# A decoder layer step: [high | low] operand for the sample tile, layer norm straight into the feed-forward accumulator, cache copy in pieces

## The chip, the core and the metric

One core of one Trainium2 chip. The time is that of one execution of the whole program on the device, in microseconds (us); a kernel's figure is the median of several runs. The engines are called as the profile calls them: PE (TensorE), PEld (its weight loads), DVE (VectorE), ACT (ScalarE), POOL (GpSimd) and SP (SyncE, which issues the DMA transfers here).

## What is computed

One inference step of a decoder trunk of one layer, for a prompt of 1024 tokens and a sample group of 8 requests with 8 new tokens each, which share the weights. All of it is float32. Cut to what matters here:

```python
x = layer_norm(x, ln_emb_g, ln_emb_b)
a_b, a_c, a_h, g_q, ..., n_kv, n_win, n_gate = split_in(x @ w_in)
...
win_all = concatenate([win_buf, win_new]); win_state = win_all[:, t:]
mix = concatenate([y_a, y_b, y_c]) @ w_out
x = layer_norm(ALPHA * x + mix, ln1_g, ln1_b)
gate, val = split(x @ w_up, 2)
gate, ffn_new = causal_dwconv(gate, ffn_buf, ffn_conv_w)
x = layer_norm(ALPHA * x + (silu(gate) * val) @ w_down, ln2_g, ln2_b)
```

The model width is 1024, the feed-forward width 2816. `win_state` of the sample group is an output of 8 x 512 rows; 504 rows of each request are a plain copy of the cache (4.03 MB in all), 8 are new.

## The kernel before

The 1088 tokens are nine tiles: tiles 0 to 7 of 128 prompt tokens and **tile 8 of the 64 sample tokens** (`rows_of`). Products are made float32-exact by splitting both operands into a high and a low part: `mm3` (L196 to L202) issues three matmuls for each 128 of the contraction, high x high (L200), low x high (L201) and high x low (L202), all into one PSUM tile. The token tile is the stationary operand in four projections, and there tile 8 has 64 stationary columns:

- `rows` in phase_a (L303 to L322), `pn`: 800 columns of w_in in natural layout, two halves of 400 columns, 8 steps of the contraction each. Its weights come in eight raw pieces (`nraw`, L288), cast to `nh` on ACT (L296) and split to `nl` on DVE or POOL (L297). `transpose_split` (L164 to L173) makes the transposed high and low operands of a token tile.
- `phase_part` (`pwq`): the first 4 of 8 contraction steps of w_out, two halves of 512 columns, run as filler within the attention part; its result goes to x_d.
- `phase_out` (`pwo`, L1607 to L1650): the other 4 steps, then the first layer norm by sums (`layer_norm_sums`, tag "1"; L143 on DVE, L144 on ACT, L145 on POOL). The result `xo` is stored to ax_d in DRAM (L1640) and transposed for the next part (`finish`, tpx).
- `down` in phase_ffn (`pd`, L1730 to L1755): w_down, two halves of 512 columns.

The feed-forward part first loads the accumulator `acc` from ax_d, a load per tile (L1668), and behind the last of these it issues the copy of the window cache to its output, one transfer of 4.03 MB from DRAM to DRAM (L1679 to L1681). It then goes over 22 blocks of 128 feed-forward channels. `up_block` makes the gate (`pug`) and value (`puv`) products in chunks of 384, 384 and 320 tokens with the weights stationary, copies the gate out of PSUM (`fg`, L1709, ACT), convolves it on DVE, and splits the product into `hh` (ACT) and `hl` (POOL, L1721). Weights come as raw tiles `wrf` (L182; cast `whf` on ACT L191, split `wlf` on POOL L192) and `wdr` (L1723; `dh`, `dl`), which share two raw buffers. After every two blocks, `down` adds both blocks' product to `acc` for tiles 0 to 8 in order: ten such groups and a last one, in which the second layer norm follows: by sums for tiles 0 to 6, and by `layer_norm_end` with a store for each half for the last two (`ENDS = 2`), tiles 7 and 8.

The order of the instructions on every engine is not the order of the source: a scheduler that simulates the engines reorders them, and each engine then works its queue in order. An issue on SP's queue also waits until one of eight semaphores is free, so until the transfer issued eight before has landed.

## Time and profile before

| | |
|---|---|
| median of three runs (lowest, highest) | 1796.55 us (1794.03, 1796.92) |
| profiled execution | 1793.5 us, of which span 1791.8 us |
| mean granted clock of PE | 0.963 |
| PE, PEld busy | 1696.1 us (95%), 1527.1 us |
| DVE, ACT, POOL busy | 918.9, 650.6, 602.2 us |
| DMA | 165.73 MB, mean 92 GB/s |

The profile is of one execution. Its busy shares are means over stages that are bound by different things: the projection from 0 to some 300 us, recurrence and attention to some 915 us, the second part of w_out to some 980 us, the feed-forward part to the end. So the table says which engine is full on the whole, and the rows by stretch, further down, say where. A granted clock of 1.00 is 2.4 GHz.

### The profile page before, as it was taken

Reading aid. Unit: us, or ns where it says so; the run is one execution under the profiler, and the core shown is the slowest. Engines: PE = TensorE matmul, PEld = TensorE weight load, DVE = VectorE, ACT = ScalarE, POOL = GpSimd, SP = SyncE. Lnnn points to the kernel's source line nnn. Section 1 sums busy time; section 2 is a strip of 40 time slices with the busy share of each in tenths; the row PEclk is TensorE's granted clock in tenths of the full one; section 3 lists DMA queues with packets and bytes.
Section 4 is the critical chain, followed back from the end, with each engine's and each line's share of the span. In section 5 each row is a group of like instructions: output and inputs, shape, how many; then the busy total and the mean of one; then the engine's idle time right before and its main releaser. Section 6 shows DMA issues by size and latency. Waiting matters only on the chain.

```text
span 1791.8 us, 26213 instructions
## 1 busy us (share of the span) xinstructions
PE 1696.1 (95%) x9759; PEld 1527.1 (85%) x9759; DVE 918.9 (51%) x2349; ACT 650.6 (36%) x1386; POOL 602.2 (34%) x487
## 2 busy tenths in 40 slices
PE   5999999988998999998799899999999999999995
PEld 4999989987867888877678899989999899899994
DVE  8334656456766677675755332332333323333338
ACT  4324542123556645555554311212113122121123
POOL 5311461232344333332545412223224132142226
PEclk8999999998679999998899999999999999999998
DMA  8412246536154553320257411102112011121102
GB/s 286 158 58 61 83 154 139 149 113 157 36 106 133 129 151 127 114 88 25 87 189 230 153 36 48 48 26 70 36 36 59 25 59 36 36 71 33 39 13 104
DMA packets 194565, 165.73 MB, mean 92 GB/s; under 512 B 60388, under 2 KB 165894, under 8 KB 194374
## 3 DMA queue, kind: packets, MB, share of 16 engines
q1 hardware_dynamic: 194438, 164.06, 31.1%
q8 instruction: 77, 1.26, 0.3%
q14 instruction: 50, 0.41, 0.1%
HBM read 121.17 MB, written 46.97 MB: 94 GB/s over the span
## 4 chain that ended last, share of the span: by engine, by line
PE 78%; DVE 7%; DMA 6%; POOL 3%; ACT 3%; issue 2%; SPq 1%; DVEq 0%; POOLq 0%; ACTq 0%
PE pd L201 5%; PE pd L202 5%; PE pd L200 5%; PE puv L201 5%; PE puv L202 5%; PE puv L200 5%; PE pug L202 4%; PE pug L201 4%; PE pug L200 4%; PE pas L1109 2%; PE pat L1168 2%; DMA wrf<-in_w_up_dram 1%; PE pao L1183 1%; PE pn L202 1%; PE pn L200 1%
## 5 line engine op out<-in xcount | busy, mean ns | idle before, releaser
L192 POOL TENSOR_TENSOR wlf<-wrf,whf 128x1024 fp32r<-128x1024 f32 x44 | 105.5, 2399 | 453.3 <-ACT whf L191 441.6
L1747 DVE TENSOR_TENSOR acc<-acc,pd 128x512 f32<-128x512 f32 x162 | 109.6, 686 | 224.6 <-PE pd L202 224.6
L1709 ACT COPY fg<-pug 128x384 f32<-128x384 f32 (+1 forms) x88 | 31.7, 388 | 431.2 <-PE pug L202 431.2
L200 PE MATMUL puv<-x1h,whf 128*128 128x384 f32 (+1 forms) x528 | 172.8, 327 | 4.2 <-ACT fg L1709 4.2
L201 PE MATMUL puv<-x1h,wlf 128*128 128x384 f32 (+1 forms) x528 | 172.8, 327 | 0.3 <-POOL wlf L192 0.3
L202 PE MATMUL puv<-x1l,whf 128*128 128x384 f32 (+1 forms) x528 | 173.0, 328 | 0.0
L200 PE MATMUL pug<-x1h,whf 128*128 128x384 f32 (+1 forms) x528 | 172.7, 327 | 0.2 <-ACT x1h L172 0.2
L201 PE MATMUL pug<-x1h,wlf 128*128 128x384 f32 (+1 forms) x528 | 172.5, 327 | 0.0
L202 PE MATMUL pug<-x1l,whf 128*128 128x384 f32 (+1 forms) x528 | 172.3, 326 | 0.0
L201 PE MATMUL pd<-dh,hl 128*128 128x512 f32 (+1 forms) x396 | 155.6, 393 | 0.0
L202 PE MATMUL pd<-dl,hh 128*128 128x512 f32 (+1 forms) x396 | 155.3, 392 | 0.0
L200 PE MATMUL pd<-dh,hh 128*128 128x512 f32 (+1 forms) x396 | 152.0, 392 | 0.8 <-DVE acc L1745 0.8
L1144 POOL TENSOR_TENSOR ass<-ass,az 128x256 f32<-128x256 f32 (+6 forms) x56 | 70.9, 1287 | 174.2 <-DVE az L1138 123.2
L1109 PE MATMUL pas<-K,aq 128*128 128x320 f32 (+5 forms) x384 | 106.2, 380 | 7.2 <-DVE amx L1116 6.6
L1179 DVE TENSOR_TENSOR atl<-pat,ath 128x512 fp32r<-128x512 f32 (+1 forms) x136 | 90.1, 668 | 31.6 <-ACT ath L1177 30.7
L200 PEld LDWEIGHTS puv<-x1h,whf 128*128 128x128 f32 x528 | 99.7, 189 | 5.5 <-ACT fg L1709 4.5
L201 PEld LDWEIGHTS pug<-x1h,wlf 128*128 128x128 f32 x528 | 99.1, 188 | 3.5
L200 PEld LDWEIGHTS pug<-x1h,whf 128*128 128x128 f32 x528 | 99.1, 188 | 2.9 <-ACT x1h L172 0.3
L202 PEld LDWEIGHTS pug<-x1l,whf 128*128 128x128 f32 x528 | 99.1, 188 | 2.9
L220 DVE SCALAR_TENSOR_TENSOR fz<-fg,w_f,fz 128x1024 f32<-128x1024 f32 x88 | 88.2, 1061 | 24.1 <-ACT fz L218 24.1
L201 PEld LDWEIGHTS puv<-x1h,wlf 128*128 128x128 f32 x528 | 99.6, 189 | 1.0 <-POOL wlf L192 0.6
L202 PEld LDWEIGHTS puv<-x1l,whf 128*128 128x128 f32 x528 | 99.5, 188 | 0.0
(554 smaller groups left out, 4264.8 us busy)
## 6 DMA issues: line engine op xcount, KB each, us to landing
wrf<-in_w_up_dram SPq DMA_DIRECT2D x44, 512.0 KB
wdr<-in_w_down_dram SPq DMA_DIRECT2D x22, 512.0 KB
aq<-q_d SPq DMA_DIRECT2D x32, 256.0 KB
wra<-in_w_in_dram SPq DMA_DIRECT2D x14, 512.0 KB
xt<-in_x_prompt_dram SPq DMA_DIRECT2D x8, 512.0 KB
x_d<-xt SPq DMA_DIRECT2D x8, 512.0 KB
sv_d<-gsv SPq DMA_DIRECT2D x8, 512.0 KB
ma_d<-gma SPq DMA_DIRECT2D x8, 512.0 KB
```

Of the source, the lines that this page charges most:

```text
L192: c.nc.gpsimd.tensor_tensor(lo, raw, hi, op=OP.subtract)
L200: c.nc.tensor.matmul(out, ah(k), bh(k), start=start and j == 0, stop=False)
L201: c.nc.tensor.matmul(out, al(k), bh(k), start=False, stop=False)
L202: c.nc.tensor.matmul(out, ah(k), bl(k), start=False, stop=stop and j == n - 1)
L220: nc.vector.scalar_tensor_tensor(o, src(i), wcol(i), o, op0=OP.mult, op1=OP.add)
L1109: nc.tensor.matmul(p[:, :step], u.q[:, h, 4 * kv + g0 + g], c.K[:, kk, ks], start=h == 0, stop=h == 1)
L1144: nc.gpsimd.tensor_tensor(x[:, g, :n], x[:, g, :n], z[:, b, g:g + 1].to_broadcast([128, n]), op=OP.mult)
L1168: nc.tensor.transpose(pt[:, a, g], (SW if b else SS)[:, g, t * 128:t * 128 + 128], c.ident)
L1179: nc.vector.tensor_tensor(tl[:, :k], pt[:, :k], th[:, :k], op=OP.subtract)
L1183: nc.tensor.matmul(po, v, tl[:, a], start=False, stop=j + a == len(steps) - 1)
L1709: nc.scalar.copy(dst, b3(p[:, o:o + m]) if three else p[:, o:o + m])
L1747: nc.vector.tensor_tensor(a, a, p[:r], op=OP.add)
```

## The change

Tile 8's four projections use one stationary operand of 128 columns, its 64 high columns followed by its 64 low ones. `mm2` multiplies it with the high and with the low part of the weights, two matmuls per step of the contraction instead of three; rows 64 to 127 of the result are the low half's share (which now also holds low x low) and are added to rows 0 to 63 afterwards. How the operand is built differs: `x8` by four POOL copies; `y_split` writes the low part next to the high one; in the feed-forward part one tile `hs` holds high, low of the sample tokens, low of the prompt, so that the low part of the last chunk takes two POOL operations (256 and 64 tokens). In `down` rows 64 to 127 of `acc`'s tile 8 gather the low half's share over all groups, and are added once, in the last.

`acc` is allocated before phase_out's last tiles, and the first layer norm writes into it; only tile 0, which runs earlier (`XB = 1`), still goes through ax_d. Eight stores and eight of the nine loads go. The cache copy is eight transfers of 504 KB, written in the source in up_block 2 to 9 and without a place to wait for. `TAIL` puts tile 8 first in each group, so the last two tiles are 6 and 7.

```diff
+TAIL = (8,) + ORDER
...
+def mm2(c, out, a, bh, bl, ks):
+    n = len(ks)
+    for j, k in enumerate(ks):
+        c.nc.tensor.matmul(out, a(k), bh(k), start=j == 0, stop=False)
+        c.nc.tensor.matmul(out, a(k), bl(k), start=False, stop=j == n - 1)
...
     # transpose_split, for tile 8 of phase_a
+        if both is not None:
+            nc.gpsimd.tensor_copy(both[:, 4 * b:4 * b + 4, 0:64], h)
+            nc.gpsimd.tensor_copy(both[:, 4 * b:4 * b + 4, 64:128], l)
...
     # rows
+                        mm2(c, p[:, :400], lambda k: x8[:, k], wh, wl, range(KD))
+                        o = nat[0:64, h * 400:h * 400 + 400]
+                        nc.scalar.copy(o, p[64:128, :400])
+                        nc.vector.tensor_tensor(o, p[0:64, :400], o, op=OP.add)
...
+def y_split(c, t, k0, pool, name):
...
+    nc.scalar.copy(h, y)
+    nc.vector.tensor_tensor(yh[:, :, 64:128] if t == 8 else yl, y, h, op=OP.subtract)
+    return yh, yl
+
+def low_rows(c, x, p, tmp, f):
+    c.nc.scalar.copy(tmp, p[64:128])
+    c.nc.vector.scalar_tensor_tensor(x[:64], x[:64], f, tmp, op0=OP.mult, op1=OP.add)
...
     # phase_part and phase_out, tile 8
+                mm2(c, p, lambda k: yh[:, k], lambda k: c.woh[k][:, n], lambda k: c.wol[k][:, n], range(4))
+                low_rows(c, x[:, n], p, ld.tile([64, 512], F32, name="xo8", tag="ln_sq", bufs=1), 1.0)
...
     # phase_out
-        layer_norm_sums(c, x, r, gB, bB, x, ld, sm, "1")
-        nc.sync.dma_start(c.ax_d[t * 128:t * 128 + r], x[:r])
+        o = c.acc[:, t] if c.xh else x
+        layer_norm_sums(c, x, r, gB, bB, o, ld, sm, "1")
+        if not c.xh:
+            nc.sync.dma_start(c.ax_d[t * 128:t * 128 + r], x[:r])
...
     # phase_ffn
-    for t in range(NT):
-        r = rows_of(t)
-        held = nc.sync.dma_start(c.acc[:r, t], c.ax_d[t * 128:t * 128 + r])
+    nc.gpsimd.memset(c.acc[64:128, 8], 0.0)
...
-        with tc.issue_after(held.ins):
-            nc.sync.dma_start(O[5][0, :, 0:504].rearrange("b t f h d -> b (t f h d)"),
-                                I["cache_nsa_win"][0, :, 8:512].rearrange("b t f h d -> b (t f h d)"))
...
     # up_block
+            if 2 <= f < 2 + NB:
+                nc.sync.dma_start(O[5][0, f - 2, 0:504].rearrange("t f h d -> t (f h d)"),
+                                  I["cache_nsa_win"][0, f - 2, 8:512].rearrange("t f h d -> t (f h d)"))
...
+            hs = hp.tile([128, T + 64 + SP], F32R, name="hs")
+            hh, hl = hs[:, :T], hs[:, T + 64:]
...
-                nc.gpsimd.tensor_tensor(hl[:, s], z[:, s], hh[:, s], op=OP.subtract)
+                m = min(t0 + n, SP)
+                nc.gpsimd.tensor_tensor(hl[:, t0:m], z[:, t0:m], hh[:, t0:m], op=OP.subtract)
+                if t0 + n > SP:
+                    nc.gpsimd.tensor_tensor(hs[:, T:T + 64], z[:, SP:], hh[:, SP:], op=OP.subtract)
...
-            return hh, hl, dh, dl
+            return hh, hl, dh, dl, hs[:, SP:SP + 128]
...
     # down
-            end = last and t >= NT - ENDS
+            end = last and t in TAIL[-ENDS:]
...
+                    mm2(c, p, lambda k: hs[k][4], wh, wl, range(len(hs)))
...
+                if last and t == 8:
+                    low = sp.tile([64, 512], F32, name="low", tag="ln_sq", bufs=1)
+                    nc.scalar.copy(low, a[64:128])
+                    a = a[0:64]
+                    nc.vector.scalar_tensor_tensor(a, a, 1.0, low, op0=OP.mult, op1=OP.add, accum_out=sm[:64, h:h + 1])
...
-            for t in range(NT):
+            for t in TAIL:
                 down(hs, t, f0 == 0, last)
```

Where the scheduler puts things now, at three places. First SP's queue in the first 40 us, before (`nraw` is a piece of the raw projection weights, `wra` one of a column block's, `xt` a token tile, `x_d` a store of a normalised tile):

```order
L182 DMA wra<-in_w_in_dram 128x8x128
L288 DMA nraw<-in_w_in_dram 128x792
L182 DMA wra<-in_w_in_dram 128x8x128
L274 DMA xt<-in_x_prompt_dram 128x1024
L279 DMA x_d<-xt 128x1024 x2
L182 DMA wra<-in_w_in_dram 128x8x128
L274 DMA xt<-in_x_prompt_dram 128x1024 x2
```

and now:

```order
L187 DMA wra<-in_w_in_dram 128x8x128
L302 DMA nraw<-in_w_in_dram 128x792
L187 DMA wra<-in_w_in_dram 128x8x128
L1739 DMA out_dram<-in_cache_nsa_win_dram 16x8064 x7
L288 DMA xt<-in_x_prompt_dram 128x1024
L1739 DMA out_dram<-in_cache_nsa_win_dram 16x8064
L293 DMA x_d<-xt 128x1024 x2
L187 DMA wra<-in_w_in_dram 128x8x128
```

All eight pieces of the cache copy, which the source writes in the feed-forward part, stand at the start, seven of them ahead of the load of token tile 5.

Second, SP's queue where the feed-forward part begins, before:

```order
L1640 DMA ax_d<-xo 128x1024
L1668 DMA acc<-ax_d 128x1024
L1676 DMA g2B<-in_ln_g_dram 128x1024
L1677 DMA b2B<-in_ln_b_dram 128x1024
L1640 DMA ax_d<-xo 128x1024
L1668 DMA acc<-ax_d 128x1024
L1640 DMA ax_d<-xo 64x1024
L1668 DMA acc<-ax_d 64x1024
L1680 DMA out_dram<-in_cache_nsa_win_dram 8x8x16128
L182 DMA wrf<-in_w_up_dram 128x8x128
```

and now:

```order
L1592 DMA yol<-y_d 128x512
L1661 DMA xo<-x_d 128x1024
L1592 DMA yol<-y_d 128x4x64
L1661 DMA xo<-x_d 64x1024
L1714 DMA g2B<-in_ln_g_dram 128x1024
L1715 DMA b2B<-in_ln_b_dram 128x1024
L187 DMA wrf<-in_w_up_dram 128x8x128
L1764 DMA wdr<-in_w_down_dram 128x1024
```

The stores to ax_d, the loads from it and the cache copy are gone from between the layer norm's loads and the weight loads.

Third, PE at the end of a group of two blocks, before (`pd` is the down-projection):

```order
L201 MATMUL puv<-x1h,wlf 128x320
L202 MATMUL puv<-x1l,whf 128x320
L200 MATMUL pd<-dh,hh 128x512
L201 MATMUL pd<-dh,hl 128x512
L202 MATMUL pd<-dl,hh 128x512
L200 MATMUL pd<-dh,hh 128x512 x2
```

and now:

```order
L206 MATMUL puv<-x1h,wlf 128x320
L207 MATMUL puv<-x1l,whf 128x320
L214 MATMUL pd<-dh,hs 128x512
L215 MATMUL pd<-dl,hs 128x512
L214 MATMUL pd<-dh,hs 128x512
L215 MATMUL pd<-dl,hs 128x512
L205 MATMUL pd<-dh,hs 128x512
L206 MATMUL pd<-dh,hs 128x512
```

The group now begins with the four matmuls of tile 8 and the first block (L214, L215 are those of `mm2`), two for each half; its second block follows some 40 rows later.

## Rows read from the trace of the kernel before

**Rows 1.** Busy us by stretch: PE, PEld, DVE, ACT, POOL; PEclk, DMA share, GB/s.

```profile
100.00:200.00 100.00, 100.00 (x600) 96.56 (x599) 52.22 (x118) 36.65 (x69) 23.71 (x26) 1.00 0.21 56
400.00:915.00 515.00, 470.45 (x2897) 392.70 (x2898) 360.30 (x1219) 280.92 (x756) 186.58 (x180) 0.90 0.39 105
1010.00:1015.00 5.00, 4.69 (x18) 4.50 (x18) 0.93 (x2) 1.30 (x4) 3.60 (x3) 0.66 0.37 109
1130.00:1500.00 370.00, 370.00 (x2027) 343.23 (x2026) 128.26 (x211) 83.12 (x136) 102.05 (x61) 1.00 0.15 45
```

**Rows 2.** Chain that ended last, 960 to 1020 us: start, us, what.

```profile
978.41 4.32 DMA ax_d<-xo
...
984.14 22.75 DMA wrf<-in_w_up_dram
1006.97 1.05 ACT whf L191
```

**Rows 3.** Timeline of PE around 1010 us: start, us, instruction, idle before it.

```profile
1009.75 0.44 PE L200 MATMUL puv<-x1h,whf 128*128 128x384 f32 x1 [4.19 <-ACT fg L1709]
...
1014.25 0.34 PE L201 MATMUL puv<-x1h,wlf 128*128 128x384 f32 x1
1014.43 0.34 PE L202 MATMUL puv<-x1l,whf 128*128 128x384 f32 x1
```

**Rows 4.** Busy us by stretch, the end (columns as in 1).

```profile
1757.00:1774.00 17.00, 16.08 (x67) 11.14 (x66) 16.63 (x32) 10.47 (x15) 16.32 (x10) 1.00 0.34 130
```

**Rows 5.** Timeline of PE, last down-projections.

```profile
1770.76 0.39 PE L202 MATMUL pd<-dl,hh 128*128 128x512 f32 x1
1770.98 0.40 PE L200 MATMUL pd<-dh,hh 128*64 128x512 f32 x1
1771.22 0.39 PE L201 MATMUL pd<-dh,hl 128*64 128x512 f32 x1
```

**Rows 6.** Groups by line and shape, weight loads: busy us, mean ns.

```profile
L202 PEld LDWEIGHTS pd<-dl,hh 128*128 128x128 f32 x352 | 66.1, 188 | 14.1
L202 PEld LDWEIGHTS pn<-nl,x0h 128*64 128x64 f32 x16 | 2.2, 135 | 0.8
```

**Rows 7.** Timeline of PE, then POOL, around tile 8's first projection.

```profile
105.37 0.34 PE L200 MATMUL pn<-nh,x0h 128*64 128x400 f32 x1
114.38 0.95 POOL L838 MEMSET gZ<- 128x1024 f32 x1 [45.01 <-PE pn L202]
```

**Rows 8.** Timeline of PE and DVE where the feed-forward part begins.

```profile
958.57 0.40 PE L202 MATMUL pwo<-wol,yoh 128*128 128x512 f32 x1
...
977.06 0.71 PE L170 MATMUL tpx<-ident,xo 64*128 64x64 f32 x8 [0.68 <-POOL xo L145]
977.98 0.42 PE L200 MATMUL pug<-x1h,whf 128*128 128x320 f32 x1 [0.21 <-ACT x1h L172]
967.91 0.68 DVE L1638 SCALAR_TENSOR_TENSOR xo<-xo,pwo 64x512 f32<-64x512 f32 x1 [1.33 <-DMA xo<-x_d]
```

**Rows 9.** Timeline of PE, then POOL, at the end of a group's up-projections.

```profile
1096.14 0.39 PE L200 MATMUL pd<-dh,hh 128*128 128x512 f32 x1
1099.89 0.87 POOL L1721 TENSOR_TENSOR hl<-fz,hh 128x320 fp32r<-128x320 f32 x1
```

**Rows 10.** Timeline of SP, ACT, POOL and PE in the first 70 us.

```profile
23.74 0.53 SPq L288 DMA_DIRECT2D nraw<-in_w_in_dram  x1
25.20 1.69 SPq L274 DMA_DIRECT2D xt<-in_x_prompt_dram  x1
31.08 0.84 ACT L296 CAST nh<-nraw 128x792 fp32r<-128x792 f32 x1
38.01 2.90 POOL L297 TENSOR_TENSOR nl<-nraw,nh 128x792 fp32r<-128x792 f32 x1
66.88 1.03 PE L170 MATMUL tpx<-ident,xt 128*128 128x128 f32 x8
```

**Rows 11.** Busy us by stretch, while the cache copy ran (columns as in 1).

```profile
990.00:994.00 4.00, 4.00 (x28) 3.90 (x27) 2.99 (x9) 1.68 (x3) 0.00 (x0) 1.00 0.60 258
```

More of the change, by code (lines that the diff above doesn't have):

```diff
@@ L161, in layer_norm_end, with transpose_split @@
         halves(n[h])
-def transpose_split(c, src, r, hi, lo, t, tag):
+def transpose_split(c, src, r, hi, lo, t, tag, both=None):
     nc = c.nc
@@ L267, in phase_a @@
             nl = wn.tile([128, KD, 800], F32R, name="nl")
+            x8 = wn.tile([128, KD, 128], F32R, name="x8")
             x_s = I["x_sample"].rearrange("b t d -> (b t) d")
@@ L1560, in out_weights @@
     eng.tensor_tensor(lo, raw, hi, op=OP.subtract)
+def y_split(c, t, k0, pool, name):
+    nc = c.nc
+    yh = pool.tile([128, 4, 128], F32R, name=f"{name}h", bufs=2)
+    yl = pool.tile([128, 4, 128], F32R, name=f"{name}l", bufs=2)
+    r = rows_of(t)
+    h = yh[:, :, :r]
+    y = yl.bitcast(F32)[:, :, :r]
+    nc.sync.dma_start(y, c.y_d[t, :, k0:k0 + 4, :r])
+    nc.scalar.copy(h, y)
[4 more added lines that the diff above has]
+    c.nc.vector.scalar_tensor_tensor(x[:64], x[:64], f, tmp, op0=OP.mult, op1=OP.add)
 def phase_part(c, I, pp):
@@ L1610, in back @@
         r = rows_of(t)
-        x = ld.tile([128, D], F32, name="xo", bufs=3)
-        nc.sync.dma_start(x[:r], c.ax_d[t * 128:t * 128 + r])
-        done.append((t, x))
+        nc.sync.dma_start(c.acc[:r, t], c.ax_d[t * 128:t * 128 + r])
+        done.append((t, c.acc[:, t]))
     for j, t in enumerate(OUT):
@@ L1738, in down @@
                 n = slice(512 * h, 512 * h + 512)
-                mm3(c, p[:r], lambda k: hs[k][0][:, s], lambda k: hs[k][1][:, s], lambda k: hs[k][2][:, n],
-                    lambda k: hs[k][3][:, n], range(len(hs)))
-                a = c.acc[:r, t, n]
+                wh, wl = lambda k: hs[k][2][:, n], lambda k: hs[k][3][:, n]
+                if t < 8:
+                    mm3(c, p, lambda k: hs[k][0][:, s], lambda k: hs[k][1][:, s], wh, wl, range(len(hs)))
+                else:
+                    mm2(c, p, lambda k: hs[k][4], wh, wl, range(len(hs)))
+                a = c.acc[:, t, n]
                 if first:
-                    nc.vector.scalar_tensor_tensor(a, a, ALPHA, p[:r], op0=OP.mult, op1=OP.add)
-                elif last:
-                    nc.vector.scalar_tensor_tensor(a, a, 1.0, p[:r], op0=OP.mult, op1=OP.add, accum_out=sm[:r, h:h + 1])
-                else:
-                    nc.vector.tensor_tensor(a, a, p[:r], op=OP.add)
+                    nc.vector.scalar_tensor_tensor(a, a, ALPHA, p, op0=OP.mult, op1=OP.add)
+                elif last and t < 8:
+                    nc.vector.scalar_tensor_tensor(a, a, 1.0, p, op0=OP.mult, op1=OP.add, accum_out=sm[:, h:h + 1])
+                else:
+                    nc.vector.tensor_tensor(a, a, p, op=OP.add)
+                if last and t == 8:
[3 more added lines that the diff above has]
+                    nc.vector.scalar_tensor_tensor(a, a, 1.0, low, op0=OP.mult, op1=OP.add, accum_out=sm[:64, h:h + 1])
                 if end:
@@ L1900, in body @@
         c.wfr = es.enter_context(tc.tile_pool(name="wfr", bufs=2, reuse_waits="tile"))
+        ap = es.enter_context(tc.tile_pool(name="acc", bufs=1, reuse_waits="tile"))
+        c.acc = ap.tile([128, NT, D], F32, name="acc")
         for _ in c.out:
@@ L1904, in body @@
         c.wop.release()
-        if "ax" in c.dbg:
-            nc.sync.dma_start(c.dbg["ax"], c.ax_d[:])
-        ap = es.enter_context(tc.tile_pool(name="acc", bufs=1, reuse_waits="tile"))
-        c.acc = ap.tile([128, NT, D], F32, name="acc")
         phase_ffn(c, I, O)
```

50 lines of the change are left out of this document (24 added, 26 removed).

## The prediction

> **What bounds the kernel now.** I read the busy time by stretch first [rows 1]. TensorE (PE) is busy all of 100 to 200 us and all of 1130 to 1500 us: a matmul taken out there is worth its own time. In the attention part, 400 to 915 us, PE works 470 of 515 us: there it is worth at most that. Two places are different. At 1010 to 1015 us the granted clock of PE is 0.66, and the timeline of PE [rows 3] shows what came before: a wait of 4.19 us on ScalarE (ACT), which copies gate chunks out of PSUM. The chain of waits [rows 2] shows who held ACT. The last layer norm's store to ax_d lands 4.32 us after its issue; the acc load behind it and the 4 MB cache copy follow on the queue of SyncE (SP); then the weight load wrf is issued at 984.14 and takes 22.75 us, and ACT's cast of these weights, ahead of the gate copies in ACT's order, begins only at 1006.97. The other such place is the end [rows 4]: from 1757 to 1774 us VectorE (DVE) works 16.63 and GpSimd (POOL) 16.32 of 17 us, PE's weight loads 11.14. The end is set by DVE and POOL, not by matmuls.
>
> **Price of a matmul.** A 512-column matmul with 128 stationary columns is followed after 0.22 us (1770.76 to 1770.98), one with 64 after 0.24 (1770.98 to 1771.22) [rows 5]: 0.23 for both. For 400 columns that is 0.23 x 400/512 = 0.18. A weight load takes 188 ns for 128 columns and 135 for 64 [rows 6], less than an interval of 0.23, so it is hidden in both forms. Two matmuls with 128 columns in place of three with 64 save a whole interval. The Trainium skill ("TensorE: Matmul & The Clock Gate", "Step-by-step: what each phase is for") says that the load's time scales with the number of stationary columns; if loads set the pace, two long ones would cost nearly what three short ones do (rival 3). The rows agree that 128 columns take longer, by 1.4 times and not twice; the equal intervals say that loads aren't the pace.
>
> **Part by part**, against the profiled execution (1793.5 us, span 1791.8), which lies 3.05 under the median of 1796.55.
> - Natural-layout projection: 8 steps by 2 halves = 16 matmuls fewer, 16 x 0.18 = **-2.9**, where PE is full. The four copies that build its operand run on POOL, which does nothing in the 45.01 us up to 114.38 [rows 7]; each has 256 elements a partition, the nearest row is 0.87 us for 320 [rows 9], so some 3.5 us in all, and PE's first use of tile 8 is at 105.37 [rows 7]: hidden. Without that cover they would cost 3.5.
> - First part of w_out: 8 fewer, 8 x 0.23 = 1.9, where PE stands still a tenth of the time for others. Bounds 0 and -1.9; in the middle, **-1.0**.
> - Second part of w_out, and the join to the feed-forward part. PE starts its last full-tile matmul at 958.57 and the 320-column up-projection, which needs tile 8, at 977.98 [rows 8]: 19.2 us after that matmul's interval ends at 958.8. Eight matmuls go (1.9), and what PE stood still in between: 0.68 for POOL, 0.21 for ACT [rows 8] and about 1 of smaller gaps. That leaves 15.4 us of PE work. Against it stands tile 8's own chain: eight transposes of tile 7 (0.7) and 16 x 0.23 of its own put the end of its matmuls at +4.4; the low half's copy and add and the two sums (0.68 each [rows 8]) about 2 more; from its sums at 967.91 + 2 x 0.68 to its transposes at 977.06 the chain took 7.8. So the transposes can start at +14.3, the chunk 0.9 later (977.06 to 977.98): +15.2, as late as PE's own work. The 1.33 us that DVE waited for xo [rows 8] go with the stores and loads of ax_d ahead of it in the queue. With two equal paths I leave half a microsecond for collisions: 19.2 to 15.9, **-3.3**, between -1.9 (matmuls alone) and -4.2 (nothing collides and the smaller gaps were larger).
> - Stall: the wait began at 1009.75 - 4.19 = 1005.56. The 14th matmul behind it starts at 1014.25; unhindered it would start at 1005.56 + 13 x 0.18 = 1007.9 (0.18 is the interval from 1014.25 to 1014.43) [rows 3]. **-6.4**, the wait and the slow matmuls. The copy and the ax_d loads no longer stand ahead of wrf; it then waits only for its raw buffer, and even 15 us after 984 would be in time for 1005. What is late next is nothing that I can see before 1060 us.
> - Down-projection: 44 fewer. 40 lie in the first ten groups, where PE is full: 40 x 0.23 = **-9.2**. The last group's four lie under DVE: 0. Tile 8 now comes first and needs the low half of the last chunk, now two POOL operations. Before, that half was ready 4.6 us after PE began the group (1096.14 to 1100.76) [rows 9]; PE now runs the first block's rows and 24 or more gate matmuls ahead of tile 8's second block, 4 x 0.23 and at least 24 x 0.18 = 5.2 us: no wait, or a few tenths. Were that cover gone, it would be up to 4.6 us for each of ten groups.
> - Tail: two more adds on DVE, of 0.68 each, where it is the bound: 1.4. The last two tiles both have 128 rows, so the last stores carry twice the bytes; against it PE is done 0.9 earlier. Bounds -1 and +3; **+1.5**.
> - Output copy: all eight pieces now stand at the program's start, right after the last piece of the raw projection weights (issued at 23.74) and a column block's, seven of them ahead of token tile 5 (issued at 25.20 [rows 10]). While the old copy ran, the DMA engines moved 258 GB/s at a busy share of 0.60 [rows 11]; 4.13 MB take 16 us at that rate. PE transposes tile 5 only at 66.88 [rows 10], 41 us after its issue: **0**, with bounds of 0 and +9 (rival 2). The Trainium skill ("DMA: Bandwidth & Descriptors", "Why a DMA increments its semaphore by 16 and not by 1") says that a transfer uses as many engines as the largest number up to 16 that divides its slowest dimensions; the share of 0.60 agrees with 8 engines for the old copy and some for other loads. By it pieces of 16 rows use all 16, and the 16 us would be an estimated 9.6.
> - Order of the attention part: scattered places differ on every engine. PE loses 45 us there [rows 1]; an eighth of it either way, -6 and +6, as bounds, taken as 0.
>
> Sum: -2.9 - 1.0 - 3.3 - 6.4 - 9.2 + 1.5 = **-21.3**; 1793.5 becomes 1772.2, and on the median 1796.55 becomes **1775**.
>
> **Rivals.**
> 1. The stall stays: another transfer is late for the same cast. For it: two raw buffers only, and ACT's order unchanged. Against it: some 15 us of slack once the copy is gone. 1775 + 6.4 = 1782.
> 2. The eight pieces choke the start. The last raw weight piece is cast at 31.08 and split on POOL at 38.01 [rows 10]; PE's first projections need it. If it took 22.75 us to land, as wrf did behind the old copy, its cast would come at 46.5, 15.4 later; less the 6.1 for which its split stood in POOL's queue (31.92 to 38.01), PE loses 9.3: 1784. **The slower side** is this mechanism at its worst: at the 109 GB/s of 1010 to 1015 us [rows 1], 4.13 MB hold the piece up for 38 us, 32 after POOL's slack: 1807. It turns slower from a delay of 6.1 + 21.3 = 27 us. Against both: the piece is issued ahead of the copies, and the rate under the old copy was 258.
> 3. Weight loads set the pace. A step then saves 3 x 135 - 2 x 188 = 29 ns instead of 180 or 230; 72 steps give 2.1 instead of 15.0 (2.9 + 1.0 + 1.9 + 9.2): 1788. The equal intervals speak against it. This is the column rule of the Trainium skill ("TensorE: Matmul & The Clock Gate", the same section) taken as the limit.
> 4. Attention's new order costs 10: 1785; or gives as much: 1765.
>
> **Numbers.** Forecast 0.60 (by itself 1769 to 1781). Stall stays 0.10; the start costs about 9 us 0.07, 27 or more 0.03; weight loads 0.04; attention +10 0.07 and -10 0.06; 0.03 for mishaps that end near no change. The range **1763 to 1787** leaves out the slowest start, the weight loads, and the far ends of attention. A change of 0.2% (3.6 us) is about what a measurement of this kernel can tell from none. Faster 0.94, same 0.03, slower 0.03.
>
> **What would show it.** Right: between 960 and 1060 us PE has no wait of over 1 us and a clock of 1.00; tile 8's matmuls come in pairs 0.23 apart; PE is as full from 40 to 100 us as before; DVE is busy nearly all of the last 35 us. Wrong: PE waiting on ACT near 1002, a gap of PE before 60 us with the copies under way, pairs wider than 0.23, PE waiting for POOL's low halves at a group's second block, or an attention part longer by more than 6 us.

## The result, and the profile after

| | before | after |
|---|---|---|
| median, four runs each (lowest, highest) | 1795.62 us (1794.03, 1796.92) | 1767.51 us (1764.39, 1772.70) |
| profiled execution, span | 1793.5, 1791.8 | 1772.7, 1771.0 |
| mean granted clock of PE | 0.963 | 0.969 |

The ratio is 0.9844, with a 95% interval of 0.9817 to 0.9870. The forecast was 1775, with 1763 to 1787 as its range. Two executions of the experiments below were disturbed (2074.03 us of e_pd3 at a mean clock of 0.741, 1868.53 of e_lndve at 0.833) and are left out of their medians. To see where the time went I cut the span at the first or last start of certain groups on PE: `pgg` (the end of the recurrence's gates), `pas` and `pcx` (attention), `pwq`, `pat` (the last attention product), the 320-token `pug` with which tile 8 enters the feed-forward part, the first `pd` and the last `puv`. Each kernel was profiled a second time (called e_before and e_after below), since two executions of one kernel differ (us; stages are worked out from the starts of the matmuls and then rounded):

| stage | before, e_before | after, e_after | mean difference |
|---|---|---|---|
| start to last `pgg` | 290.8, 290.3 | 288.3, 287.2 | -2.8 |
| to first `pas` | 150.8, 152.2 | 154.3, 151.1 | +1.2 |
| to last `pcx` | 179.4, 174.0 | 165.3, 168.3 | **-9.9** |
| to last `pwq` | 125.4, 125.0 | 130.3, 129.1 | +4.5 |
| to last `pat` | 166.6, 165.7 | 162.9, 163.1 | -3.2 |
| to the 320-token `pug` | 65.0, 65.3 | 66.7, 66.2 | +1.3 |
| to the first `pd` | 45.9, 45.8 | 41.9, 40.9 | -4.4 |
| to the last `puv` | 722.9, 722.9 | 714.1, 714.1 | -8.8 |
| to the end of the span | 45.1, 45.1 | 47.2, 47.1 | +2.1 |

The stages sum to -20; the medians are 28 apart, to which I come back.

Busy time by stretch of the changed kernel (columns as in [rows 1]: stretch, its length, busy us of PE, PEld, DVE, ACT and POOL with instruction counts, granted clock, DMA share, GB/s):

```profile
100.00:200.00 100.00, 100.00 (x601) 98.74 (x601) 55.35 (x126) 37.51 (x70) 24.50 (x27) 1.00 0.21 56
400.00:915.00 515.00, 469.97 (x2943) 391.52 (x2943) 362.62 (x1230) 286.21 (x763) 193.09 (x184) 0.93 0.41 110
...
960.00:965.00 5.00, 3.64 (x24) 3.29 (x22) 1.70 (x3) 3.48 (x7) 2.30 (x2) 1.00 0.00 0
965.00:970.00 5.00, 3.34 (x15) 3.16 (x16) 1.78 (x4) 2.16 (x5) 3.91 (x2) 0.67 0.00 0
970.00:975.00 5.00, 5.00 (x22) 5.00 (x22) 0.00 (x0) 0.00 (x0) 0.00 (x0) 0.65 0.36 105
1000.00:1010.00 10.00, 10.00 (x63) 9.96 (x62) 5.45 (x9) 3.78 (x7) 5.12 (x3) 1.00 0.20 54
1130.00:1500.00 370.00, 370.00 (x2040) 347.89 (x2039) 120.13 (x202) 84.19 (x138) 105.15 (x74) 1.00 0.15 45
...
1734.00:1751.00 17.00, 14.10 (x60) 10.58 (x59) 15.56 (x30) 9.57 (x14) 16.30 (x9) 1.00 0.30 100
```

PE is still full where it was full. The stall is gone: at 1000 to 1010 us PE works 10.00 of 10 at a clock of 1.00. In its place stands one at 960 to 975 us, PE idle for 3.0 of 10 us and then at a clock of 0.65. The end is still POOL's (16.30 of 17) and DVE's, answering to [rows 4]. The waits of PE from 900 to 1060 us (us in all, times, the longest) name the new one, and a smaller one ahead of it; the timelines of PE, DVE, POOL and ACT around it tell its story:

```profile
PE tpx L171 <- POOL acc L146: 3.0, 1, 3.0
PE pwo L205 <- DVE xo L1676: 1.5, 2, 1.1
```

```profile
948.53 0.39 PE L207 MATMUL pwo<-wol,yoh 128*128 128x512 f32 x1
...
966.62 1.11 PE L171 MATMUL tpx<-ident,acc 64*128 64x64 f32 x8 [2.99 <-POOL acc L146]
967.77 0.64 PE L205 MATMUL pug<-x1h,whf 128*128 128x320 f32 x1
...
969.11 0.52 PE L207 MATMUL puv<-x1l,whf 128*128 128x384 f32 x1
969.43 0.52 PE L205 MATMUL puv<-x1h,whf 128*128 128x384 f32 x1
```

```profile
948.96 0.69 DVE L1676 SCALAR_TENSOR_TENSOR xo<-xo,pwo 128x512 f32<-128x512 f32 x1 [1.42 <-PE pwo L207]
...
952.98 0.68 DVE L1601 SCALAR_TENSOR_TENSOR xo<-xo,xo 64x512 f32<-64x512 f32 x1
...
955.16 2.51 DVE L1601 SCALAR_TENSOR_TENSOR xo<-xo,xo 64x512 f32<-64x512 f32 x1 [0.78 <-ACT xo L1600]
957.77 0.68 DVE L1676 SCALAR_TENSOR_TENSOR xo<-xo,pwo 64x512 f32<-64x512 f32 x1
```

```profile
948.27 2.39 POOL L146 TENSOR_TENSOR acc<-xo,b1B 128x1024 f32<-128x1024 f32 x1 [1.27 <-ACT xo L145]
...
954.74 2.39 POOL L146 TENSOR_TENSOR acc<-xo,b1B 128x1024 f32<-128x1024 f32 x1 [1.26 <-ACT xo L145]
...
964.22 2.35 POOL L146 TENSOR_TENSOR acc<-xo,b1B 64x1024 f32<-64x1024 f32 x1 [1.26 <-ACT xo L145]
```

```profile
953.50 1.15 ACT L145 ACTIVATE xo<-xo,rs 128x1024 f32<-128x1024 f32 x1 [1.17 <-POOL rs L143]
954.56 0.57 ACT L1600 COPY xo<-pwo 64x512 f32<-64x512 f32 x1
```

The same add of tile 8's low half took 0.68 us for one half of the columns and 2.51 for the other, which began while POOL was adding the bias of tile 7 (954.74 to 957.13) and ended 0.5 us after that. In all eight profiles of the changed kernel and its variants in which such a low add began beside a bias add of POOL, it took 2.22 to 2.51 us; wherever it did not, 0.68. An add with one input in PSUM (L1676) took 0.69 even within such a bias add (948.96, POOL 948.27 to 950.66). The Trainium skill ("SBUF — State Buffer", "Who interferes with whom") says that a DVE instruction with two inputs in SBUF contends with a GpSimd instruction that reads SBUF; these rows agree. By the rows the price was 1.8 us on the path to the feed-forward part. A second delay lies just ahead of it: tile 8's last matmul in w_out was done at 953.37, but the copy of its low half on ACT (L1600) began only at 954.56, behind tile 7's L145; the first half's copy had begun 0.25 us after its matmuls, so this cost 0.9.

### The profile page after: what moved, and what is told of

Read it like the earlier page. It is cut to its first block, busy times and chain, and to the rows that moved or that the text cites. A ratio compares the mean times of both kernels' runs of the same rounds, so it can differ in the third digit from the quotient of the medians.

```text
span 1771.0 us, 26112 instructions
## 1 busy us (share of the span) xinstructions
PE 1672.2 (94%) x9683; PEld 1517.0 (86%) x9683; DVE 914.5 (52%) x2357; ACT 655.0 (37%) x1392; POOL 608.4 (34%) x514
## 4 chain that ended last, share of the span: by engine, by line
PE 79%; DVE 9%; DMA 5%; ACT 3%; issue 3%; SPq 1%; POOL 1%; DVEq 0%; ACTq 0%; POOLq 0%
PE puv L207 5%; PE puv L205 5%; PE puv L206 5%; PE pug L205 5%; PE pug L206 5%; PE pug L207 5%; PE pd L206 4%; PE pd L205 4%; PE pd L207 4%; PE pas L1130 2%; PE pat L1189 2%; PE pao L1204 1%; PE pjg L207 1%; PE pjg L206 1%; PE pjg L205 1%
## 5 line engine op out<-in xcount | busy, mean ns | idle before, releaser
L205 PE MATMUL pd<-dh,hs 128*128 128x512 f32 x352 | 138.2, 393 | 3.5 <-DVE acc L1789 3.1
L206 PE MATMUL pd<-dh,hs 128*128 128x512 f32 x352 | 138.2, 393 | 0.0
L207 PE MATMUL pd<-dl,hs 128*128 128x512 f32 x352 | 138.1, 392 | 0.0
L1130 PE MATMUL pas<-K,aq 128*128 128x320 f32 (+5 forms) x384 | 102.5, 369 | 7.1 <-DVE amx L1137 6.3
L1768 POOL TENSOR_TENSOR dl<-wdr,dh 128x1024 fp32r<-128x1024 f32 x22 | 52.8, 2398 | 155.3 <-ACT dh L1767 155.3
L233 DVE SCALAR_TENSOR_TENSOR fz<-fg,w_f,fz 128x1024 f32<-128x1024 f32 x88 | 89.0, 1060 | 25.6 <-ACT fz L231 25.6
```

Of the source, the lines that this page charges most:

```text
L205: c.nc.tensor.matmul(out, ah(k), bh(k), start=start and j == 0, stop=False)
L206: c.nc.tensor.matmul(out, al(k), bh(k), start=False, stop=False)
L207: c.nc.tensor.matmul(out, ah(k), bl(k), start=False, stop=stop and j == n - 1)
L233: nc.vector.scalar_tensor_tensor(o, src(i), wcol(i), o, op0=OP.mult, op1=OP.add)
L1130: nc.tensor.matmul(p[:, :step], u.q[:, h, 4 * kv + g0 + g], c.K[:, kk, ks], start=h == 0, stop=h == 1)
L1768: nc.gpsimd.tensor_tensor(dl, raw, dh, op=OP.subtract)
```

## The experiments

Kernels that start with e_ are changes of the changed kernel, unless the text says that the kernel before was changed. Medians stand with the lowest and the highest time, and with the ratio to the kernel before, run beside them, and its 95% interval.

**The changed kernel again (e_after), without an edit.**

> The changed kernel once more, unaltered. The profiled execution was at the top of its four runs (1772.7 against a median of 1767.5), and its parts differ from what was forecast: from the first score matmul (pas, 442.6 us) to the last cached-page transpose (pcx, 608) it took 14 us less than the kernel before, and the stretches at half clock between 440 and 500 us were shorter. Theory 1 (the low clock of PE decides the spread): the time lies between 1764 and 1773 us; the part from pas to the last pcx differs from the first profile by some us, together with the granted clock there, while the other parts (0 to 290 us, the 19 us from the last w_out matmul to the 320-column up-projection, the 47 us from the last up-projection to the end) stay within 1 us. Theory 2 (the new order of instructions made that part shorter by itself): it has the same length within 1 us again, and the spread comes from elsewhere.

Measured: 1765.29 us (1760.83 to 1768.87), ratio 0.9836 (0.9802 to 0.9870). The gain stands, and the stages of the table repeat within 3.3 us. Neither theory fits whole: from `pas` to `pcx` it took 168.3 instead of 165.3 at nearly the same clock (0.87 and 0.88).

**The kernel before again (e_before), one execution.**

> The kernel before, unaltered, for a second profile. In its first one the part from the first score matmul (pas) to the last cached-page transpose (pcx) took 179 us, in five profiles with other orders 165 to 171, and the granted clock from 480 to 500 us was 0.54 against 0.83 to 0.89. Theory 1 (its order of instructions there is the slower one): 176 to 182 us again, with a low clock there again. Theory 2 (the first profile was an unlucky execution): 165 to 172 us, and a time near the lower end of its runs (1782).

Measured: 1787.96 us. From `pas` to `pcx` it took 174.0, between the two theories, at a clock of 0.87 where the first profile had 0.81. The stall is there again, with the same owner and length (waits of PE, 940 to 1040 us):

```profile
PE puv L200 <- ACT fg L1709: 4.1, 1, 4.1
```

### The copy and the stall

**One copy of 4 MB, late, in the changed kernel (e_latecopy).**

```diff
-            if 2 <= f < 2 + NB:
-                nc.sync.dma_start(O[5][0, f - 2, 0:504]...)
...
-        nc.sync.dma_start(bB, bcast(I["ln2_b"][0], D))
+        held = nc.sync.dma_start(bB, bcast(I["ln2_b"][0], D))
+        with tc.issue_after(held.ins):
+            nc.sync.dma_start(O[5][0, :, 0:504]..., I["cache_nsa_win"][0, :, 8:512]...)
```

> The changed kernel with one edit: the cache copy is again one transfer, issued behind the loads of the second layer norm's gain and bias, ahead of the weight load wrf, as in the kernel before. Theory 1 (the copy alone held up wrf and so made the stall at 1005 us): PE waits some 4 us on ACT's gate copy near 1000 us again, with half clock behind it; 5 to 7 us slower than the changed kernel, some 1773. Theory 2 (the chain through ax_d made wrf late, and the copy is hidden without it): no wait of PE over 1 us there, and the time of the changed kernel within 2 us.

Measured: 1779.42 us (1775.80 to 1787.30), ratio 0.9930 (0.9901 to 0.9959). The stall did not come back, yet the kernel lost 14 us. SP issued the copy at 961.88 and `wrf` at 977.33; the stage from the 320-token `pug` to the first `pd` was 40.9, as in e_after. The loss lies ahead of the copy: of the 10.9 us between its profile and e_after's, 8.4 lie from `pas` to the last `pat` (468.9 instead of 460.5) and 2.9 between `pgg` and `pas`. So neither theory holds. The scheduler had moved matmuls there (952 in place of 931 between `pas` and `pcx`).

**The same order of PE, with a copy ahead of wrf (e_stall).** It adds work that the kernel doesn't need: a store of tile 8's normalised rows and a copy of the cache to scratch memory.

```diff
+        held = nc.sync.dma_start(c.ax_d[SP:], c.acc[:64, 8])
+        with tc.issue_after(held.ins):
+            nc.sync.dma_start(c.cp_d[:], I["cache_nsa_win"][0, :, 8:512]...)
```

> The changed kernel with the old situation at the start of the feed-forward part put back, and nothing else: a store of tile 8's normalised rows to ax_d, and behind it one transfer of the cache's 4.03 MB, to a scratch tensor, just ahead of the weight load wrf on SP's queue (the eight pieces at the start stay; the order on PE is the same throughout). The late copy of the run before stood there too, but was issued 15 us earlier, since no store had to be waited for, and there was no stall. Theory 1 (wrf is late when the copy starts just ahead of it): wrf takes some 20 us to land, PE waits some 4 us for ACT near 1000 us, with slow matmuls behind; 41 us from the first 320-column gate matmul to the first down-projection become 46 to 47, and the time is 5 to 6.5 us above the changed kernel (1765 to 1767). Theory 2 (ACT's order or the buffers made the stall in the kernel before, and the copy was only there too): 41 us again, and the same time within 2 us.

Measured: 1765.63 us (1761.37 to 1767.50), ratio 0.9832 (0.9790 to 0.9874): no cost. SP and ACT of e_stall:

```profile
963.33 0.78 SPq L1718 DMA_DIRECT2D cp_d<-in_cache_nsa_win_dram  x1
965.15 0.39 SPq L187 DMA_DIRECT2D wrf<-in_w_up_dram  x1
```

```profile
987.24 1.05 ACT L196 CAST whf<-wrf 128x1024 fp32r<-128x1024 f32 x1 [5.46 <-DMA wrf<-in_w_up_dram]
...
989.72 0.85 ACT L1750 COPY fg<-pug 128x384 f32<-128x384 f32 x2
```

`wrf` behind the copy takes 22 us, as in [rows 2], and ACT waits 5.46 us for it; but PE doesn't wait for ACT, because the load was issued 1.4 us after the 320-token `pug` (963.8 us) and not 6.2 us after it, as before (984.14 against 977.98): 4.8 us earlier, where the wait had been 4.2. So the copy alone does not make the stall; it needs the late issue of `wrf` behind the chain of ax_d store and `acc` load too.

**The kernel before, with the eight early pieces in place of its copy (e_bcopy).**

```diff
-        with tc.issue_after(held.ins):
-            nc.sync.dma_start(O[5][0, :, 0:504]..., I["cache_nsa_win"][0, :, 8:512]...)
...
+            if 2 <= f < 2 + NB:
+                nc.sync.dma_start(O[5][0, f - 2, 0:504]..., I["cache_nsa_win"][0, f - 2, 8:512]...)
```

> The kernel before with one edit: the cache copy in eight pieces, which the scheduler puts at the program's start as in the changed kernel; acc still goes through ax_d. Theory 1 (the stall needs the copy just ahead of wrf): no wait of PE over 1 us near 1005 us; the 45.8 us from the first 320-column gate matmul to the first down-projection become 39 to 41, and the start is no longer: 5 to 7 us faster there than the kernel before. Its attention part has another order than both kernels', which can add or take some 10 us: so the stretches decide, not the total. Theory 2 (the loads of ax_d hold wrf up by themselves): a wait of 2 us or more stays.

Measured: 1783.92 us (1780.63 to 1793.28), ratio 0.9951 (0.9926 to 0.9977). SP and ACT:

```profile
978.70 0.45 SPq L1668 DMA_DIRECT2D acc<-ax_d  x1
979.20 0.58 SPq L182 DMA_DIRECT2D wrf<-in_w_up_dram  x1
```

```profile
989.80 1.04 ACT L191 CAST whf<-wrf 128x1024 fp32r<-128x1024 f32 x1
```

The chain of stores and loads is as before, `wrf` is issued as late as before (5.9 us after the `pug` at 973.3), and without the copy its cast has no wait: the stage of the stall falls from 45.8 to 39.3, **-6.5**, with the same order of PE and a clock of 1.00 in place of 0.96. So the late issue alone does not make the stall either. The start costs nothing (289.8 against 290.3). The other stages moved as well (`pcx` to `pwq` 137.6, `pwq` to `pat` 151.4), since the schedule did.

### The matmul pairs

**Three matmuls for tile 8 in the down-projection (e_pd3).**

```diff
-                    mm2(c, p, lambda k: hs[k][4], wh, wl, range(len(hs)))
+                    mm3(c, p[:64], lambda k: hs[k][0][:, s], lambda k: hs[k][1][:, s], wh, wl, range(len(hs)))
...
-                if last and t == 8:
-                    low = sp.tile([64, 512], F32, name="low", tag="ln_sq", bufs=1)
```

> The changed kernel with the down-projection of tile 8 as before: three matmuls with 64 columns per step, no low half in acc, one POOL operation for the low part of the last chunk; tile 8 still first in every group. The order on PE is the same up to the feed-forward part. Theory 1 (a matmul costs its interval of 0.23 us in both forms): 40 x 0.23 = 9.2 us more between the first down-projection and the last value matmul (714 us become 723), and about 1.5 less at the end without the two adds: 7 to 9 us slower than the changed kernel. Theory 2 (weight loads set the pace, so that a step saves 29 ns): 1.2 us more in that stretch, and no slower on the whole.

Measured: 1772.74 us (1770.44 to 1782.31), ratio 0.9893 (0.9842 to 0.9943). The stage up to the last `puv` is 723.0 (before 722.9), **8.9** us longer than in the changed kernel, or 0.22 for each of 40 matmuls. The timeline of PE within a group shows one interval for both forms, in e_pd3 (64 columns) and in the changed kernel (128):

```profile
1299.90 0.39 PE L206 MATMUL pd<-dh,hl 128*64 128x512 f32 x1
1300.13 0.39 PE L207 MATMUL pd<-dl,hh 128*64 128x512 f32 x1
1300.36 0.40 PE L206 MATMUL pd<-dh,hl 128*64 128x512 f32 x1
```

```profile
1295.40 0.39 PE L214 MATMUL pd<-dh,hs 128*128 128x512 f32 x1
1295.63 0.39 PE L215 MATMUL pd<-dl,hs 128*128 128x512 f32 x1
1295.87 0.40 PE L214 MATMUL pd<-dh,hs 128*128 128x512 f32 x1
```

**Three matmuls in the first part of w_out (e_part3).**

```diff
-            if t < 8:
-                mm3(c, p, ...)
-            else:
-                mm2(c, p, ...)
-                low_rows(c, x, p, ..., ALPHA)
+            mm3(c, p[:r], lambda k: yh[:, k, :r], lambda k: yl[:, k, :r], ...)
```

> The changed kernel with one part undone: the first part of w_out (phase_part) multiplies tile 8 by three matmuls of 64 columns again. The order on PE is the changed kernel's up to the last cached-page transpose (pcx) and exactly the order of the kernel before from there to the last matmul of phase_part. So far that first stretch (from the first score matmul) took 165 to 171 us in six profiles with the changed kernel's order and 174 and 179 with the order before; the next (to the last matmul of phase_part) 128 to 130 and 125. Theory 1 (the order that the scheduler makes decides the length of these stretches): 165 to 171 us in the first and 125 to 126 in the second, and with the third (to the last transpose of the attention part) as long as before, 165 to 166, some 0 to 2 us slower than the changed kernel in all. Theory 2 (the 8 matmuls decide): the second stretch becomes 1.9 us longer than in the changed kernel, 131.

Measured: 1768.17 us (1762.09 to 1770.85), ratio 0.9849 (0.9820 to 0.9877), whose interval covers e_after's ratio. Up to the last `pcx` PE's order is the changed kernel's, and the stage is the changed kernel's too (168.7). From there to the last `pwq` it is exactly the order of before, and the stage is 125.7 (before 125.4 and 125.0, after 130.3 and 129.1), with eight matmuls **more** than after; the next stage is 165.5 (165.7 to 166.6 before). What is lost in one stage is won in the other: the order only moved work across `pwq`. Over both stages it is 291.2 with the eight matmuls, and 290.7 to 293.2 in the seven profiles that have the changed kernel's order there: no gain from the pairs shows.

### The join

**Tile 8 ahead of the prompt tiles in w_out (e_out8).**

```diff
-OUT = ORDER + (8,)
+OUT = (0, 8) + ORDER[1:]
```

> The changed kernel with one edit: phase_out takes tile 8 second, OUT = (0, 8, 1, ..., 7). Theory 1 (tile 8's own chain of low copy, add and layer norm ends the join, where the forecast 3.3 us were lost): with tile 7 last, 8.4 us of its chain lie under 48 gate matmuls (8.3 us), the join has 16 x 0.23 = 3.7 us less after tile 7 and no wait of 3.0; about 4.5 to 5 us are won, and 2 more if PE then doesn't fall to 1.2 GHz behind it: 6 us less than the changed kernel, some 1761. Theory 2 (ACT and POOL need their 6 us per tile whatever the order, so that the wait only moves to another tile): within 1 us of the changed kernel.

Measured: 1767.36 us (1762.41 to 1770.31), ratio 0.9852 (0.9817 to 0.9886). PE's wait on POOL is gone, and so is the half clock behind it (39.7 to the first `pd`); in its place PE waits 1.2 us for DVE's `x1l` and 1.4 for ACT's `x1h` of the last prompt tile. The stages from `pat` to `pd` sum to 105.3 against e_after's 107.1, but the whole is no faster than e_after (1765.29): as the second theory says, the wait only moved.

**The layer norm through ax_d again, pairs and early copy kept (e_axd).**

```diff
-        o = c.acc[:, t] if c.xh else x
-        layer_norm_sums(c, x, r, gB, bB, o, ld, sm, "1")
+        layer_norm_sums(c, x, r, gB, bB, x, ld, sm, "1")
+        nc.sync.dma_start(c.ax_d[t * 128:t * 128 + r], x[:r])
...
+    for t in range(NT):
+        nc.sync.dma_start(c.acc[:r, t], c.ax_d[t * 128:t * 128 + r])
```

> The changed kernel with one part undone: the first layer norm goes through ax_d again, eight stores and nine loads; the cache copy stays at the start, the pairs of tile 8 stay. The order on PE is nearly the same. Theory 1 (writing into acc directly is worth nothing by itself once the cache copy is out of the way, since wrf, behind the stores and loads, then lands in a few us): no stall near 1000 us, and the time of the changed kernel within 2 us. Theory 2 (the loads in the queue make xo or wrf late, which the direct way saves): the wait of PE before tile 8's transposes grows from 3.0 by 1 us or more, or wrf makes PE wait again; 2 to 6 us slower.

Measured: 1776.30 us (1773.63 to 1780.23), ratio 0.9905 (0.9874 to 0.9936), 11 above e_after. PE's waits from 900 to 1060 us:

```profile
PE tpx L171 <- POOL xo L146: 4.2, 1, 4.2
PE pug L205 <- DVE xo L1677: 1.9, 1, 1.9
```

The stage from `pat` to `pug` takes 69.3, 3.1 more than in e_after; another 4.7 comes from `pwq` to `pat`, where PE's order differs. So the direct accumulator is worth 3 in that stage; what it frees upstream comes through the order. The two profiles are 6.5 apart, so that 4.5 of the 11 can't be placed.

**The bias of the last two tiles' first layer norm added on DVE (e_lndve).**

```diff
-        layer_norm_sums(c, x, r, gB, bB, o, ld, sm, "1")
+        layer_norm_sums(c, x, r, gB, bB, o, ld, sm, "1", nc.vector if t in (7, 8) else None)
```

> The changed kernel with one edit: the last addition of the first layer norm (b1B) is made by DVE instead of POOL for tiles 7 and 8. In the changed kernel the low half's add on DVE took 2.51 us instead of 0.68 while POOL made this addition for tile 7 (2.39 us), and PE waited 3.0 us for POOL's addition for tile 8, with slow matmuls behind. Theory 1 (DVE and POOL hold each other up there, and this lengthens tile 8's chain): the low add takes 0.7, tile 8's chain is 2 to 3 us shorter, the wait of 3.0 goes or falls under 1 us, PE stays at full clock: the stretch from the last w_out matmul to the first down-projection (56 us) is 3 to 5 us shorter, 1760 to 1762 where the changed kernel took 1765 to 1767. Theory 2 (the chain is bound by its length on ACT and PE, or the slow add has another cause): the wait stays at 2 us or more, and the time is the same within 2 us.

Measured: 1759.65 us (1753.55 to 1766.46), ratio 0.9809 (0.9771 to 0.9847). The slow add and most of the wait are gone, as the first theory says (DVE, then PE's wait):

```profile
950.45 1.23 DVE L146 TENSOR_TENSOR acc<-xo,b1B 128x1024 f32<-128x1024 f32 x1 [0.31 <-ACT xo L145]
951.59 0.68 DVE L1601 SCALAR_TENSOR_TENSOR xo<-xo,xo 64x512 f32<-64x512 f32 x1
```

```profile
...
PE tpx L171 <- DVE acc L146: 0.5, 1, 0.5
```

The bias add takes 1.23 on DVE instead of 2.39 on POOL, the low half's add 0.68 again, and PE waits 0.5 instead of 3.0. From the end of tile 8's last matmul in w_out to the end of its sums it takes 4.3 us instead of 5.0, since the bias add now stands ahead of the low add on DVE; from there to its transposes 6.5 instead of 8.2. So on the path 0.7 us are won up to the sums, and 1.7 come from the shorter bias add and from DVE's order behind the sums. The stage to `pug` falls to 63.9 and the next to 39.3 (no half clock): 2.3 and 1.6 less than e_after, 3.9 together. The median lies 5.6 under e_after's, but the intervals of the two ratios overlap: shown in its place, not yet on the whole.

### The end

**Tile 8 last in each group (e_tail8), and this with the add on DVE (e_lndve_t8).**

```diff
-TAIL = (8,) + ORDER
+TAIL = ORDER + (8,)
```

> The changed kernel with one edit: down takes tile 8 last again (TAIL = ORDER + (8,)), so that the last two tiles are 7 and 8 as before. The stretch from the last up-projection matmul to the end was 44.9 us before and 47.0 in the changed kernel, where 1.5 had been forecast. Theory 1 (two more adds on DVE, which is the bound there): the order matters little, 46 to 48 us again. Theory 2 (the order costs, by two last tiles of 128 rows and their stores): 45 us or less, 2 us faster than the changed kernel. Beside it, the pairs of tile 8 come last in every group, which should cost nothing.

> The edit of e_lndve together with tile 8 last in down (as in e_tail8, whose last 46.5 us were 0.6 shorter than the 47.1 of the changed kernel). Theory 1: both add up, 0.5 to 1 us below e_lndve in the profile's last stretch, about 1760. Theory 2: tile 8's combination at the very end takes back what the shorter stores give, and the time is e_lndve's.

Measured: e_tail8 1765.27 us (1755.78 to 1767.70), ratio 0.9831 (0.9794 to 0.9868); e_lndve_t8 1760.61 us (1759.49 to 1765.78), ratio 0.9823 (0.9792 to 0.9853). The stage behind the last `puv` takes 46.45 in both against e_after's 47.14: the order of the tiles is worth 0.7. e_pd3, which has no low half to add at the end, takes 45.55, so the two adds and their copies cost 1.6. e_lndve_t8 can't be told from e_lndve, and its interval overlaps e_after's.

## Why the prediction was right, and where it was not

**Natural-layout projection: right.** Forecast -2.9. Tile 8's matmuls there, where PE is full, start over 5.68 us (105.67 to 111.35) instead of 8.55 (105.37 to 113.92), which is -2.9; the stage up to the last `pgg` gained 2.8. The copies that build the operand are hidden, as the POOL row of the changed kernel shows: done by 98.55 us, while PE first uses the operand at 105.67.

```profile
97.11 0.75 POOL L177 CAST x<-x0h 128x256 fp32r<-128x256 f32 x2 [16.94 <-ACT x0h L173]
97.80 0.75 POOL L178 CAST x<-x0l 128x256 fp32r<-128x256 f32 x2
```

**First part of w_out: not seen.** The -1.0 does not show in e_part3, and lies within what the order does around it.

**Join: wrong.** "**-3.3**, between -1.9 (matmuls alone) and -4.2" did not come. From the end of the last full-tile matmul's interval to the 320-token `pug` it took 19.0 us after (948.76 to 967.77; 18.8 in e_after) and 19.2 before (19.6 in e_before). PE's own work did shrink, but tile 8's chain did not let the transposes start at +14.3: they began at +17.9 (966.62). The steps that failed are "the low half's copy and add and the two sums (0.68 each [rows 8]) about 2 more" and "I leave half a microsecond for collisions". Tile 8's matmuls ended at +4.6 as forecast (+4.4), but copy, add and sums took 5.0 us (953.37 to 958.38) and not 2. The collision of DVE's low add with POOL's bias add is 1.8 of that, and it is one that the change makes: before there was no low half to add there. The second low copy's wait behind tile 7 on ACT is another 0.9. From the sums to the transposes it took 8.2 instead of the 7.8 before. PE's pause then brought the half clock behind it, 2.1 us that I had not counted (41.4 to the first `pd` in the mean, 39.3 in e_lndve and e_bcopy). Ahead of the join, from the last `pat` to the last full-tile matmul, the changed kernel takes 1.8 more in the mean; PE waits there 1.5 and 1.2 us for DVE's sums (L1676), and in the kernel before 0.5 and 0.3 for DVE. I had no term for that, and why DVE is later was not tried. e_lndve takes the collision and POOL's longer add away and wins 3.9 in place; no run removes the collision alone.

**Stall: right, the mechanism half.** "-6.4" was the forecast, and e_bcopy measures -6.5 (45.8 to 39.3), where the copy is all that was changed in the source and PE's order in this stage is the same. In the changed kernel the stage gained 4.4, because the half clock of the join falls into it. I named the copy and the ax_d loads together; e_stall and e_bcopy show that either one alone would not have stalled PE. Rival 1 falls.

**Down-projection: right.** Forecast -9.2, measured -8.8, and 8.9 in e_pd3 backwards. No wait for the low halves on POOL shows in the full stretch (370.00 of 370). Rival 3 falls: with weight loads as the pace the ten groups would have given 40 x 29 = 1.2 us. That is the column rule of the Trainium skill ("TensorE: Matmul & The Clock Gate", "Step-by-step: what each phase is for") taken as a limit, which is rival 3's reading and not the page's; the trace agrees that more columns load longer (188 against 135 ns) and speaks against the limit, since 64 and 128 columns have the same interval of 0.23.

**Tail: right.** Forecast +1.5, between -1 and +3; measured +2.1, of which 1.6 by e_pd3 are the adds, and the rest is the order, 0.5 in e_pd3 against before and 0.7 by e_tail8.

**Copy at the start: right.** Rival 2 falls. SP spent 5.65 us on issuing seven pieces, and tile 5's load follows at 30.91 instead of 25.20, but the raw weights' cast came at 30.68 (31.08 before) and PE transposed tile 5 at 67.19 (66.88 before). From 32 to 36 us the DMA engines were busy for a share of 0.99 and moved 347 GB/s (0.45 and 184 before). Where SP issues the pieces:

```profile
24.67 5.65 SPq L1739 DMA_DIRECT2D out_dram<-in_cache_nsa_win_dram  x7
30.91 0.34 SPq L288 DMA_DIRECT2D xt<-in_x_prompt_dram  x1
```

**Order of the attention part: the bound taken for the value.** "-6 and +6, as bounds, taken as 0": from the first `pas` to the last `pat` the two profiles of after are 8.5 under those of before, in the mean, of which at most 1.8 are the eight matmuls of `pwq`. That is beyond the bound of -6: rival 4 on its good side. Two things lie in it, and the rows separate them. From first `pas` to last `pcx` in before, e_before, after and e_after:

```profile
441.60:621.00 179.40, 166.45 (x932) 138.49 (x932) 122.61 (x437) 104.65 (x337) 70.55 (x87) 0.81 0.45 106
```

```profile
442.50:616.50 174.00, 157.97 (x931) 130.74 (x931) 122.47 (x437) 104.24 (x336) 70.16 (x87) 0.87 0.45 108
```

```profile
442.60:607.90 165.30, 153.89 (x932) 128.82 (x932) 118.90 (x437) 104.39 (x336) 70.85 (x87) 0.88 0.50 115
```

```profile
438.30:606.60 168.30, 155.69 (x931) 130.05 (x931) 119.06 (x437) 104.30 (x336) 70.87 (x87) 0.87 0.47 111
```

The same matmuls (931 or 932) keep PE busy for 166 us at a clock of 0.81 and for 154 to 158 at 0.87 or 0.88. Between the two executions of before 8.5 us of busy time go with the clock, at an equal program and order; 3.1 less of idle time in the slower one leave 5.4. Between e_before and the two of after, at an equal clock, 3.2 are busy time and 4.0 idle time (16.0 against 11.4 and 12.6): that is order. In ten of the eleven profiles of the changed kernel and its variants (all but e_latecopy) PE's order in this stage is the same, matmul for matmul. Nine of them, at a clock of 0.87 or 0.88, have 165.0 to 168.7 us; e_tail8, at 0.84, has 171.6. The order of before has 174.0 at 0.87 and 179.4 at 0.81, and e_bcopy, with a third order, 175.6 at 0.89. Which part of the change the scheduler answered to was not settled. The early copy alone does not bring this order (e_bcopy), and without the early copy it is another one again (e_latecopy, 170.7); the direct accumulator (without it 165.2) and the pairs of `pd` and of `pwq` (without them 165.0 and 168.7) are not needed for it.

**The sum: in part luck.** With the terms as measured in the profiles the gain is 20, with the medians 28; the forecast was 21.3. But 8.5 of the 20 come from attention's order, which the forecast took as 0. The other stages gained 11.4, where their terms (without the first part of w_out) were 20.3: the join and what lies ahead of it came out 4.6 worse, the stall 2.0, four smaller differences make up the rest. Of the signs of being right, the pairs 0.23 apart came, and PE was as full from 40 to 100 us as before (59.5 of 60 us in both); "no wait of over 1 us and a clock of 1.00" between 960 and 1060 us did not.

The 8 us between 20 and 28 are spread between executions. In 52 executions of the kernel before, over four comparisons, the time goes with the mean granted clock: 0.958 at 1807.35 us, 0.971 at 1781.98, a correlation of -0.88, and some 1.4 us for each 0.001. Their mean clock is 0.966, and that of e_after's six is 0.9705. The two profiled executions of before lie 3.3 us under the mean of the 52, and those of after 4.4 above the mean of its ten, and that is the 8 us; in which stages the other executions differ no trace shows. Whether the change raises the clock in attention or only removes the two places where it fell is open. The forecast's own range, 1769 to 1781, missed the median by 1.5 us; the wider range held it.

## What to carry to other kernels

Where an engine is full, price a removed matmul by the interval to the next one in the trace; it held within 0.4 us over 40 of them. Where two paths meet (here PE's own work and one tile's chain through DVE, ACT and POOL), look at what the change puts beside what on DVE and POOL before counting a gain, and give a pause of PE the slow matmuls behind it as well. Ahead of a stage full of small dependent steps, the schedule's answer to a change elsewhere can be worth as much as the change: give it a range of its own, and compare two profiles of each kernel before assigning the difference. And add up the measured terms one by one: a total within the range can hide a term that failed behind one that nobody forecast.
